# First x rows cast by POOL's queue, and inner products 1 and 5 of four stages split a third time

## The chip, the cores and the metric

The kernel runs on one core of one Trainium2 chip. The time is the device time of one execution in microseconds (us); of three runs the median is 1380.51 us. Five engines work side by side, each on its own instructions in program order, and wait for each other through semaphores: TensorE (PE in the profile, with PEld for loading the stationary operand), VectorE (DVE), ScalarE (ACT), GpSimd (POOL) and SyncE (SP). POOL, SP and ACT also issue the transfers (DMA). Transfers that change the type on their way, from 32-bit to 16-bit floats, are issued by POOL.

## The reference

```python
batch, seq, hidden, n_experts, expert_hidden = 16, 512, 512, 8, 2048
logits_max = np.max(router_logits, axis=-1, keepdims=True)
probs = np.exp(router_logits - logits_max)
probs = probs / np.sum(probs, axis=-1, keepdims=True)
output = np.zeros((batch, seq, expert_hidden), dtype=np.float32)
for e in range(n_experts):
    expert_out = np.matmul(x, expert_weights[e])
    output += probs[:, :, e:e+1] * expert_out
```

That is one product: the left side has 8192 rows and 8 x 512 columns, in which expert e's block is x times that expert's probability; the right side stacks the eight experts' weights to 4096 x 2048.

## The kernel before

**Two levels of splitting.** The product is cut in two along rows, depth and columns, and each such 2 x 2 x 2 cut is done with 7 products instead of 8, from sums and differences of blocks (Strassen's scheme in Winograd's form). The outer level has the products r = 1, 2, 5, 6, 7, 4, 3, each over 16 pieces q of 256 rows, with a depth of 4 experts x 512 and 1024 columns. `product(r, q)` is one such piece. The inner level cuts the piece again: 128 rows, a depth of 1024 (8 chunks of 128, K8), 512 columns (one PSUM bank). Its 7 inner products come in the order `STEPS = (1, 5, 6, 2, 7, 3, 4)`. An inner product is a step of 8 matmuls, each 128 x 128 by 512 columns, that add up in one bank. The 512 rows of the first two pieces of product 1 are computed plainly at the start (lines 316 to 340).

**Stages.** A stage is one or two pieces (`add(...)`, lines 716 to 743), and `run(stage)` (line 689) interleaves their steps: 1a 1b 5a 5b 6a 6b 2a 2b 7a 7b 3a 3b 4a 4b, fourteen slots. Stages 0 to 3 hold pairs of product 1, stages 4 to 9 one of product 2 and one of product 1, stages 10 to 14 pairs of product 2. Two pieces of a stage that belong to one product share the right factor.

**What VectorE does.** For a piece, `Left` makes z (x times probabilities, line 430; twice, for k = 0 and 1), the difference s2 (tile d) and i (from z and d, for inner products 7 and 3). `Right` makes differences of the weights, 128 x 4096 each. After a step, `post` empties or copies the bank: on ScalarE copies, on VectorE additions to a base. A piece of product 2 adds to kept rows: its bases are fetched into the h tiles (12 buffers), or, for q of 9 and more, are the outputs of product 1 still in them. In bank terms inner product 1 ends in bank x, which `post(1)` copies (product 1) or adds to its base (product 2) into bank b; 6, 7 and 4 go on in x, 5 and 3 in bank q, 2 in b.

**What sets the order.** Every instruction from line 342 on is kept in program order. The program itself decides when VectorE does a task: `later(cost, make)` appends to one queue, `slack()` after each step runs tasks while a modelled VectorE clock is behind a modelled TensorE clock, and `need(task)` runs everything queued up to a task that the next step reads. Hooks (`at(stage, slot, make)`) start loads of weights and queue tasks at a slot: in stage 11 from slot 6 `odd_t` queues three weight differences of 2.29 each (line 873), in stages 4 to 9 `wedge_at` queues three of 1.22. Input rows are begun two stages ahead (`start_loads`) and finished by transposing transfers on SP's queue (`finish_loads`).

**The start.** The first 1024 rows of x are in xs0 as 16-bit floats. Its first half comes as 32-bit rows through ScalarE's and SyncE's queues (line 86) and is cast by ScalarE and VectorE (`cast_x32`, line 301); the second half (`cast_x`, line 199) and the weights b11 come through POOL's queue, which casts. `early_z0` multiplies a row block by a diagonal of probabilities on TensorE. Ten matmuls on zeros run ahead of it.

Of the kernel before, what the change touches and what calls it, by code (L numbers as in the profile page):

```python
# [31 lines left out]
def kernel(  # L32
# [7 lines left out]
    nc = tc.nc  # L40
    P = 128
    f16 = mybir.dt.float16
# [64 lines left out]
    def dve(i):  # L107
        last[i.ins.engine] = i.ins
        tc.keep_in_program_order(i)
# [28 lines left out]
    def new_w():  # L138
        return wpool.tile([P, K8, NB], f16, name="w", tag="w")
# [59 lines left out]
    def cast_x(j):  # L199
# [4 lines left out]
    nc.gpsimd.affine_select(out=ident, in_=ident, compare_op=mybir.AluOpType.is_equal, fill=0.0, base=0,  # L204
                            pattern=[[-1, P]], channel_multiplier=1)
    b11 = {kn: new_w() for kn in BLOCKS}
    with behind():
        for kn in BLOCKS[:3]:
            cast_block(11, kn, b11[kn], 2 if kn == (0, 0) else 1)
# [88 lines left out]
                for c in (2 * g, 2 * g + 1) for j in (2 * h, 2 * h + 1)]  # L298
    ORDERS = [(c, j) for c in range(C) for j in range(4)], QUARTERS

    def cast_x32(j):
        if j % 2:
            dve(nc.vector.tensor_copy(xs0[:, j, :], x32[:, j, :]))
        else:
            act(nc.scalar.copy(xs0[:, j, :], x32[:, j, :]))  # L305

    ds_ = [diag_e(0)]
    for h in range(2):
        for j in (2 * h, 2 * h + 1):
            cast_x32(j)  # L310
# [70 lines left out]
    def evacuated():  # L381
        clock["dve"] = max(clock["dve"], clock["pe"]) + 0.69


    x_dram = {}
# [48 lines left out]
    class Left:  # L434
# [6 lines left out]
        def make(self, k):  # L441
            if self.of is not None:
                need(self.of.task[k])
            t = self.t[k] = new_z()
            times(t, k, self.xb, self.pb)
            if self.less is not None:
                u = new_u()
                times(u, k, *self.less)
                tt(t, t, u, SUB)
            if self.of is not None:  # L450
                tt(t, self.of.t[k], t, SUB)
# [99 lines left out]
                tt(o[tn], q if p in (5, 3) else x, o[tn], ADD)  # L551


    def out_rows(q, odd, cols, tn):
        t, n = tn
        return out_f[ds((2 * q + odd) * HQ + t * HP, HP), ds(cols * NH + n * NB, NB)]
# [127 lines left out]
    def queue_lefts(stage):  # L684
        if stage < len(stages):
            for p in stages[stage]:
                queue_left(p.left)

    def run(stage):
        some = stages[stage]  # L690
        for p in some:
            p.left.queue_i()
        n = 0
        for i in range(len(STEPS)):
            for p in some:
                for make in hooks.get((stage, n), ()):
                    make()
                p.step(p.steps[i])
                slack()
                p.post(p.steps[i])  # L700
                n += 1
                if n == 1:
                    queue_lefts(stage + 1)
                if n == late.get(stage, 1):
                    start_loads(stage + 2)
                if n == 5:
                    store_loads(stage + 1)
                if n == 7:
                    finish_loads(stage + 2)

    def fetch_at(stage, slot, base, *tns):
        for tn in tns:
# [334 lines left out]
```

## Time and profile before

| what | us |
|---|---|
| runs: median, lowest, highest | 1380.51, 1379.98, 1381.56 |
| span of the profiled execution | 1380.8 |
| TensorE busy in it | 1370.6 |
| VectorE busy in it | 1109.4 |
| ScalarE, POOL busy in it | 184.2, 410.8 |

The profile gives the span, from the first instruction to the last, as the profiled execution's own time; it lies within the three runs' times. In its rows, a row of the timeline reads: start, duration, engine, line, operation, output tile and input tiles, shapes, count, and in brackets how long the engine had been idle and what ended that. A row of the windows reads: the stretch, its length, each engine's busy time with the number of instructions, the clock that was granted to TensorE (1.00 is full), the transfers' share and their GB/s. A group's row reads: line, engine, operation, tiles, shapes, count, then busy time in us and the mean of one in ns, then the idle time ahead of them.

### The profile page before, as it was taken

To read this page: it belongs to the slowest core of one execution; us is meant where nothing else is said; L and a number is where in the kernel's file an instruction comes from. 1 tells how busy PE (TensorE), PEld (TensorE's weight loads), DVE (VectorE), ACT (ScalarE), POOL (GpSimd) and SP (SyncE) were. 2 spreads that over 40 slices of the span, in tenths; PEclk is the share of its full clock that TensorE was granted. 3 is DMA by queue.
4 is the path that set the end of the run, shared out by engine and by line. 5 is a ranking of instruction groups with operands and counts; after the bars stand their busy time and mean duration, and the time that the engine had idled before them with its cause. 6 is when DMAs were issued, how large, how long until landed. Compare 5 with 4: busy or idle time off the path is not lost.

```text
span 1380.8 us, 17496 instructions
## 1 busy us (share of the span) xinstructions
PE 1370.6 (99%) x6394; PEld 622.9 (45%) x6394; DVE 1109.4 (80%) x1292; ACT 184.2 (13%) x319; POOL 410.8 (30%) x650
## 2 busy tenths in 40 slices
PE   8999999999999999999999999999999999999998
PEld 4444444444444444444444444444444444444444
DVE  5755767769889888789897988889889898898782
ACT  3222111100001111111111100000000000222221
POOL 2122323231223233343332122233333322232321
PEclk9999999999999999999999999999999999999999
DMA  9898999999897998899897998988898979998785
GB/s 194 200 267 196 222 226 279 239 299 370 241 339 231 285 297 261 260 263 250 259 268 267 327 402 216 224 235 211 232 233 229 238 214 313 225 199 184 166 150 99
DMA packets 191287, 338.54 MB, mean 245 GB/s; under 512 B 52961, under 2 KB 87009, under 8 KB 187489
## 3 DMA queue, kind: packets, MB, share of 16 engines
q0 software_dynamic: 88400, 184.59, 55.1%
q1 hardware_dynamic: 98480, 123.86, 30.8%
q10 hardware_dynamic: 4320, 28.98, 5.3%
q8 instruction: 50, 0.82, 0.3%
q14 instruction: 37, 0.29, 0.1%
HBM read 207.65 MB, written 156.43 MB: 264 GB/s over the span
## 4 chain that ended last, share of the span: by engine, by line
PE 91%; issue 4%; DMA 2%; POOL 1%; DVE 1%; ACT 0%; ACTq 0%; POOLq 0%; DVEq 0%
PE ps L134 91%; DMA out_dram<-h 1%; POOL out_dram L128 1%; DVE h L114 1%; DMA x<-in_x_dram 0%; POOL wd L128 0%; DVE z L114 0%; DVE u L114 0%; DVE z L234 0%; ACT w L305 0%; DVE h L188 0%; DVE h L189 0%; DVE h L184 0%; ACT h L186 0%; ACT z L232 0%
## 5 line engine op out<-in xcount | busy, mean ns | idle before, releaser
L134 PE MATMUL ps<-w,z 128*128 128x512 f16 x5416 | 1179.3, 379 | 1.7 <-DVE h L114 1.7
L134 PEld LDWEIGHTS <-z 128*128 128x128 f16 x5416 | 530.1, 98 | 639.7 <-issue 4.5
L128 POOL DMA_DIRECT2D out_dram<-h x380 | 248.9, 676 | 748.6 <-ACT h L544 373.3
L114 DVE TENSOR_TENSOR h<-ps,h 128x512 f32<-128x512 f32 x415 | 282.3, 687 | 210.3 <-PE ps L134 189.6
L114 DVE TENSOR_TENSOR z<-xT,pT 128x2048 f16<-128x2048 f16 x220 | 266.8, 1216 | 11.6 <-DMA xT<-xs 7.2
L134 PE MATMUL ps<-w,d 128*128 128x512 f16 x880 | 199.1, 379 | 0.0
L134 PEld LDWEIGHTS <-d 128*128 128x128 f16 x880 | 86.1, 98 | 103.8
L114 DVE TENSOR_TENSOR z<-z,d 128x2048 f16<-128x2048 f16 x110 | 132.1, 1215 | 0.0
L114 DVE TENSOR_TENSOR w<-w 128x1024 f16<-128x1024 f16 (+2 forms) x92 | 100.8, 1102 | 4.5 <-DMA wd<-w 2.7
L533 ACT COPY h<-ps 128x512 f32<-128x512 f32 x90 | 52.8, 586 | 374.6 <-PE ps L134 321.5
L544 ACT COPY h<-ps 128x512 f32<-128x512 f32 x64 | 37.5, 586 | 486.0 <-PE ps L134 435.6
L114 DVE TENSOR_TENSOR d<-z 128x1024 f16<-128x1024 f16 x110 | 75.3, 685 | 6.8 <-PE ps L134 5.0
L114 DVE TENSOR_TENSOR z<-z,u 128x2048 f16<-128x2048 f16 x64 | 78.4, 1225 | 2.2
L114 DVE TENSOR_TENSOR u<-xT,pT 128x2048 f16<-128x2048 f16 x64 | 77.9, 1217 | 0.0
L530 ACT COPY h<-ps 128x512 f32<-128x512 f32 x90 | 52.8, 587 | 173.9 <-PE ps L134 162.5
L128 POOL DMA_DIRECT2D wd<-w x86 | 48.3, 584 | 35.3 <-DVE w L114 26.2
L128 POOL DMA_DIRECT2D w<-in_expert_weights_dram x65 | 49.1, 784 | 32.4 <-DMA wd<-w 22.6
L114 DVE TENSOR_TENSOR ps<-ps,h 128x512 f32<-128x512 f32 (+1 forms) x66 | 45.3, 688 | 12.6 <-PE ps L134 12.6
L128 POOL DMA_DIRECT2D kept<-h x56 | 30.9, 551 | 77.1 <-ACT h L533 48.3
L114 DVE TENSOR_TENSOR h<-h 128x512 f32<-128x512 f32 (+2 forms) x69 | 45.0, 674 | 0.1
L526 ACT COPY ps<-ps 128x512 f32<-128x512 f32 x45 | 25.6, 570 | 114.6 <-PE ps L134 114.6
L114 DVE TENSOR_TENSOR z<-z 128x2048 f16<-128x2048 f16 x32 | 39.2, 1225 | 1.1
(51 smaller groups left out, 101.2 us busy)
## 6 DMA issues: line engine op xcount, KB each, us to landing
out_dram<-h POOLq DMA_DIRECT2D x380, 256.0 KB, 6.2
pT<-p_dram SPq DMA_DIRECT2D x140, 256.0 KB, 6.0
w<-wd ACTq DMA_DIRECT2D x27, 1024.0 KB, 9.7
h<-kept SPq DMA_DIRECT2D x100, 256.0 KB, 5.6
xT<-x SPq DMA_DIRECT2D x87, 256.0 KB, 5.7
wd<-w POOLq DMA_DIRECT2D x72, 256.0 KB, 5.6
w<-in_expert_weights_dram POOLq DMA_DIRECT2D x35, 512.0 KB, 10.1
h<-out_dram SPq DMA_DIRECT2D x68, 256.0 KB, 5.1
```

What stands on the lines that cost most here:

```text
L114: dve(nc.vector.tensor_tensor(out=o, in0=a, in1=b, op=op))
L128: note(nc.gpsimd.dma_start(out=o, in_=i, **how))
L134: note(nc.tensor.matmul(ps, z, w, start=start, stop=stop, skip_group_check=True))
L526: act(nc.scalar.copy(self.banks["b"], x))
L530: act(nc.scalar.copy(o[tn], q if p == 5 else x))
L533: act(nc.scalar.copy(o[TN[p]], b if p == 2 else x))
L544: act(nc.scalar.copy(o[tn], b))
```

## The change

Two things are changed.

The first half of xs0 is loaded by two casting transfers of POOL's queue, ahead of the weights; the 32-bit tile, its two transfers and its four casts are gone.

In stages 2 and 3 (product 1) and 11 and 12 (product 2) the two pieces' inner products 1 and 5 are done together. The two pieces' row blocks are the two halves of the rows, the depth of 8 chunks is cut in 4 and 4, the 512 columns in 256 and 256, and the 8 block products are replaced by 7 parts of 4 matmuls of 128 x 128 by 256 columns. `Split` makes the four differences of the right factor for each of the two inner products (tile t, once for the two stages), `Third` the four sums of the left side (tile s, for each stage). Within the banks, parts 1 and 5 fill the two halves of the second piece's bank; ScalarE copies one half into the first piece's bank and the other into an h tile; parts 2, 6, 7, 3 and 4 add to halves, and after 6 and 7 VectorE adds 256 columns from a bank and the h tile into a bank. The last two steps (4a, 4b) of the stage ahead are held back and run between the parts; the four posts of 1 and 5 follow the last part. The left sides of such a stage are made in another order: both first z, the four s, both d, both second z.

```diff
-    x32 = wpool.tile([P, 4, H], f32, name="x32", tag="w")
...
-        begin.dma_start(out=x32[:, ds(2 * q, 2), :], in_=x_f[rows, :].rearrange("(p j) h -> p j h", p=P))
...
+    for q in range(2):
+        pool(xs0[:, ds(2 * q, 2), :], x_f[ds(2 * q * HQ, HQ), :].rearrange("(p j) h -> p j h", p=P))
     with behind():
...
-    def cast_x32(j):
-        if j % 2:
-            dve(nc.vector.tensor_copy(xs0[:, j, :], x32[:, j, :]))
-        else:
-            act(nc.scalar.copy(xs0[:, j, :], x32[:, j, :]))
...
+    class Split:
...
+        def make(self, p, i):
+            if i == 0:
+                self.t[p] = wpool.tile([P, 4, C, HQ], f16, name="t", tag="w")
+            w, t = self.right.op(p), self.t[p]
+            block = lambda k, n: w[:, ds(k * C, C), COLS[n]]
+            x, y = ((block(0, 1), block(0, 0)), (block(1, 1), t[:, 0]), (block(1, 1), block(0, 1)),
+                    (block(1, 0), t[:, 1]))[i]
+            tt(t[:, i], x, y, SUB)
...
+    class Third:
...
+        def make(self, i):
+            if i == 0:
+                self.s = wpool.tile([P, 4, C, HQ], f16, name="s", tag="w")
+            s, (a, b) = self.s, (p.left.t[0] for p in (self.a, self.b))
+            lo, hi = ds(0, C), ds(C, C)
+            x, y = ((b[:, lo], b[:, hi]), (s[:, 0], a[:, lo]), (b[:, hi], s[:, 1]), (a[:, hi], s[:, 1]))[i]
+            tt(s[:, i], x, y, ADD if i == 0 else SUB)
...
+        def part(self, p, m):
+            n = "xq"[THIRD.index(p)]
+            if m == 1:
+                self.b.banks[n] = bank()
+            ya, yb = self.a.banks.get(n), self.b.banks[n]
+            z, w = self.op(p, m), self.split.op(p, m)
+            o = {1: (yb, 0), 5: (yb, 1), 2: (ya, 0), 6: (yb, 0), 7: (yb, 0), 3: (ya, 1), 4: (yb, 0)}[m]
+            for c in range(C):
+                mm(o[0][:, COLS[o[1]]], z[:, c], w[:, c], m == 1 and c == 0, c == C - 1)
+            clock["pe"] += 0.44
+            if m == 5:
+                ya = self.a.banks[n] = bank()
+                act(nc.scalar.copy(ya[:, COLS[0]], yb[:, COLS[0]]))
+                self.t5[n] = h_tile([P, HQ], f32)
+                act(nc.scalar.copy(self.t5[n], yb[:, COLS[1]]))
+            elif m in (6, 7):
+                evacuated(0.42)
+                tt((ya if m == 6 else yb)[:, COLS[1]], yb[:, COLS[0]], self.t5[n], ADD)
...
+    def run_third(stage):
+        t = thirds[stage]
+        before(stage, 0)
+        t.parts("x1", "x5", "q1", "q5")
+        after(stage, 1)
+        before(stage, 1)
+        held.pop(0)()
+        after(stage, 2)
+        t.parts("x2", "q2", "x6", "q6")
+        before(stage, 2)
+        held.pop(0)()
+        after(stage, 3)
+        before(stage, 3)
+        t.parts("x7", "q7", "x3", "q3", "x4", "q4")
+        for p in THIRD:
+            for product in (t.a, t.b):
+                product.post(p)
+        after(stage, 4)
...
+    for stage in (2, 3):
+        third(stage, 1)
+    at(1, 2, splits[1].queue)
+    for stage in (11, 12):
+        third(stage, 2)
+    at(10, 2, splits[2].queue)
```

In the names of the parts, x stands for inner product 1 and q for inner product 5, and the digit is the part. With the change the program has 96 matmuls more (224 of 256 columns for 128 of 512), VectorE has 48 operations more and two casts fewer, ScalarE 16 copies of 256 columns more, two casts and one transfer fewer, POOL two transfers more, SyncE one fewer.

More of the change, by code (lines that the diff above doesn't have):

```diff
@@ L379, in slack, with evacuated @@
             queue.popleft().run()
-    def evacuated():
-        clock["dve"] = max(clock["dve"], clock["pe"]) + 0.69
+    def evacuated(cost=0.69):
+        clock["dve"] = max(clock["dve"], clock["pe"]) + cost
     x_dram = {}
@@ L682, in queue_left, with third, before, after @@
             left.queue_make(1)
-    def queue_lefts(stage):
-        if stage < len(stages):
+    thirds, splits, held = {}, {}, []
+    def third(stage, r):
+        if r not in splits:
+            splits[r] = Split(right[r])
+        thirds[stage] = Third(*stages[stage], splits[r])
+    def queue_lefts(stage):
+        if stage in thirds:
+            two = [p.left for p in stages[stage]]
+            for left in two:
+                left.queue_make(0)
+            thirds[stage].queue_sums()
+            for left in two:
+                left.queue_s2()
+            for left in two:
+                left.queue_make(1)
+        elif stage < len(stages):
             for p in stages[stage]:
                 queue_left(p.left)
+    def before(stage, n):
+        for make in hooks.get((stage, n), ()):
+            make()
+    def after(stage, n):
+        if n == 1:
+            queue_lefts(stage + 1)
+        if n == late.get(stage, 1):
+            start_loads(stage + 2)
+        if n == 5:
+            store_loads(stage + 1)
+        if n == 7:
+            finish_loads(stage + 2)
+    def run_third(stage):
[12 more added lines that the diff above has]
+        t.parts("x7", "q7", "x3", "q3", "x4", "q4")
+        for p in THIRD:
+            for product in (t.a, t.b):
+                product.post(p)
+        after(stage, 4)
     def run(stage):
@@ L692, in run, with one @@
             p.left.queue_i()
[L693 to L709, printed above, removed]
+        slots = [(p, i) for i in range(len(STEPS)) for p in some]
+        def one(n):
+            p, i = slots[n]
+            before(stage, n)
+            p.step(p.steps[i])
+            slack()
+            p.post(p.steps[i])
+            after(stage, n + 1)
+        first = 0
+        if stage in thirds:
+            run_third(stage)
+            first = 4
+        end = len(slots) - (2 if stage + 1 in thirds else 0)
+        for n in range(first, end):
+            one(n)
+        for n in range(end, len(slots)):
+            held.append(lambda n=n: one(n))
     def fetch_at(stage, slot, base, *tns):
```

31 lines of the change are left out of this document (29 added, 2 removed).

## The prediction

> **What bounds the kernel now.** I read the page's busy times first, then its chain of waits, then TensorE's groups by form.
>
> ```profile
> span 1380.8 us, 17496 instructions
> PE 1370.6 (99%) x6394; PEld 622.9 (45%) x6394; DVE 1109.4 (80%) x1292; ACT 184.2 (13%) x319; POOL 410.8 (30%) x650
> PE 91%; issue 4%; DMA 2%; POOL 1%; DVE 1%; ACT 0%; ACTq 0%; POOLq 0%; DVEq 0%
> ...
> L134 PEld LDWEIGHTS <-z 128*128 128x128 f16 x5416 | 530.1, 98 | 639.7 <-issue 4.5
> ```
>
> ```profile
> L134 PE MATMUL ps<-w,z 128*128 128x512 f16 x5400 | 1177.5, 379 | 1.7 <-DVE h L114 1.7
> L134 PE MATMUL ps<-w,z 128*128 128x256 f16 x16 | 1.9, 273 | 0.0
> ```
>
> TensorE is busy 99% of the span, and the 5400 large matmuls waited 1.7 us in all. So the end moves by what is added to TensorE's row of work: columns taken out, waits put in. VectorE, at 80%, sets nothing now, but it works in program order, and the change gives it more to do. Where that matters is a question of single stages, so I read windows of one stage's length: one around stage 2, and three across stages 10 to 12.
>
> ```profile
> core 0: us, PE busy (x) PEld busy (x) DVE busy (x) ACT busy (x) POOL busy (x), PEclk, DMA share, GB/s
> 87.00:111.00 24.00, 24.00 (x113) 10.92 (x112) 10.97 (x13) 5.83 (x10) 6.63 (x11) 1.00 1.19 256
> 279.00:303.00 24.00, 24.00 (x113) 10.84 (x111) 18.34 (x23) 1.76 (x3) 9.09 (x15) 1.00 1.10 317
> 303.00:327.00 24.00, 24.00 (x113) 10.90 (x112) 17.91 (x22) 1.17 (x2) 5.89 (x10) 1.00 1.11 312
> 327.00:351.00 24.00, 24.00 (x113) 10.88 (x112) 22.05 (x24) 1.18 (x2) 4.87 (x9) 1.00 1.00 391
> ```
>
> The reader is to see that TensorE has no gap in any of them, and that VectorE has 13 us free around stage 2, 6 us in stages 10 and 11, and 2 us in stage 12. The span is 0.3 us above the median of the runs, 1380.51, so I add changes to the median.
>
> **Columns taken out.** The diff puts four stages (2, 3, 11, 12) on the new scheme, two inner products each: 8 times, two steps of 8 matmuls 512 wide become 7 parts of 4 matmuls 256 wide. One step's length is the distance between VectorE's releases by TensorE near the end; a 256-wide matmul's pitch comes from the group of 16 above.
>
> ```profile
> 1371.81 0.69 DVE L114 TENSOR_TENSOR h<-ps,h 128x512 f32<-128x512 f32 x1 [1.98 <-PE ps L134]
> 1373.54 0.69 DVE L114 TENSOR_TENSOR h<-ps,h 128x512 f32<-128x512 f32 x1 [1.04 <-PE ps L134]
> 1375.26 0.69 DVE L114 TENSOR_TENSOR h<-ps,h 128x512 f32<-128x512 f32 x1 [1.03 <-PE ps L134]
> ```
>
> A step is (1375.26 - 1371.81)/2 = 1.73 us. The 16 matmuls took 1.9 us with the last one's 0.273 in it, so the pitch is (1.9 - 0.273)/15 = 0.108 and a part is 0.43 us. 8 x (2 x 1.727 - 7 x 0.434) = 3.3 us. That group is only 16 matmuls; at a pitch of 0.110 it would be 3.0. I take -3.2, between -3.0 and -3.4.
>
> **What VectorE and ScalarE get.** 16 differences of weights (t), 16 sums of the left side (s) and 16 additions of 256 columns. Prices, as pitch from start to start in a row without idle time:
>
> ```profile
> 295.12 0.69 DVE L114 TENSOR_TENSOR h<-ps,h 128x512 f32<-128x512 f32 x1 [2.73 <-DMA kept<-h]
> 295.73 0.68 DVE L114 TENSOR_TENSOR d<-z 128x1024 f16<-128x1024 f16 x1
> 296.33 0.68 DVE L114 TENSOR_TENSOR h<-ps,h 128x512 f32<-128x512 f32 x1
> 296.93 1.22 DVE L114 TENSOR_TENSOR z<-xT,pT 128x2048 f16<-128x2048 f16 x1
> 298.06 0.68 DVE L114 TENSOR_TENSOR h<-ps,h 128x512 f32<-128x512 f32 x1
> ...
> 327.36 2.28 DVE L114 TENSOR_TENSOR w<-w 128x4096 f16<-128x4096 f16 x1
> ...
> 1365.69 0.76 DVE L114 TENSOR_TENSOR ps<-ps,h 128x256 f32<-128x256 f32 x2 [3.30 <-PE ps L134]
> 1377.01 0.37 ACT L999 COPY h<-ps 128x256 f32<-128x256 f32 x1 [12.42 <-PE ps L134]
> ```
>
> 0.60 for a t, an s or an evacuation h; 1.13 for a product z; 2.20 for a weight sum w (its 2.28 less the 0.08 by which the others overlap); 0.38 for an addition of 256 columns: 32 x 0.60 + 16 x 0.38 = 25 us in all. ScalarE's 16 copies of 0.37 us fall where it is busy 1.2 to 5.8 us in 24; each has a whole held step (1.73 us) before a part needs it. These cost nothing unless h buffers are late. What counts is when TensorE next needs VectorE, and for that I walk the changed program's order with these pitches.
>
> **Stages 2 and 3: no wait.** VectorE makes the second z of stage 2 when its x lands (78.97, below); behind it now stand 4 s, 2 d, 2 z, 6 t and 4 evacuations, and 2 z for stage 2. The pitches sum to 17.1, so the first 256-wide addition can start at 96.1. TensorE ended stage 1's last step before the new parts at 90.2; four parts, a held step, four parts and a held step later, 97.1, it needs that addition, 0.4 us long. Cover: 0.6 us. If the x landed more than 0.6 us later, the rest would go on the path.
>
> ```profile
> 78.97 1.23 DVE L114 TENSOR_TENSOR z<-xT,pT 128x2048 f16<-128x2048 f16 x1 [5.17 <-DMA xT<-xs]
> 90.27 0.69 DVE L114 TENSOR_TENSOR h<-ps,h 128x512 f32<-128x512 f32 x1 [1.04 <-PE ps L134]
> ```
>
> **Stage 11, first use of t for product 5: +1.0.** Before stage 11 VectorE waits for a store of kept rows until 295.12. From there the changed order is
>
> ```
> h(5a) z h(5b) s h(6a) s h(6b) s s d d z z h(7a) t h(7b) t h(3a) t t h(3b) t'
> ```
>
> that is 18 x 0.605 + 3 x 1.13 = 14.3 us up to the first t', which ends at 310.1. TensorE's stage 10 has its first step's end at 288.83, so its twelfth ends at 288.83 + 11 x 1.727 = 307.8, and after three parts, at 309.1, it asks for t'. Wait 1.0. Even without the wait for the store, h(3a) can't start before its step ends at 306.1, and five operations from there end at 309.3: at least 0.2. A store 0.5 us later makes it 1.5.
>
> ```profile
> 288.83 0.70 DVE L114 TENSOR_TENSOR ps<-ps,h 128x512 f32<-128x512 f32 x1 [0.49 <-PE ps L134]
> ...
> 335.99 1.22 DVE L114 TENSOR_TENSOR z<-z,d 128x2048 f16<-128x2048 f16 x1
> ```
>
> **Stage 12: +0.3 and +3.0.** The three weight sums of the odd block (2.28 us each, queued in stage 11) now don't fit there and slip past the third split. Before, the z that products 7 and 3 need was made at 335.99, as the stage began, the weight sums done in the stage ahead. In the changed order one sum stands between the additions of parts 6 and 7: from the end of q6, 0.05 + 0.36 + 2.20 + 0.61 + 0.40 = 3.6, against 1.73 + 4 x 0.43 = 3.46 until x4 needs it: 0.2, and 0.1 more at the next step. The other two stand between the evacuation of 6b and that z: from the end of 6b, 0.05 + 0.61 + 2.31 + 2.20 + 1.22 = 6.4 us, while TensorE has only 2a and 2b, 3.45 us, before 7a needs the z. Wait 3.0. This hangs on no transfer: the evacuation itself waits for TensorE, so nothing earlier can shrink it. Queued behind are 7a and everything after it. One stage later the same order leaves TensorE ahead of every wait by my walk.
>
> **The clock after a 3 us wait: +1.5.** At the start of the kernel the granted clock fell after a patchy stretch:
>
> ```profile
> 7.27 0.62 PE L134 MATMUL ps<-h,w 128*128 128x128 f16 x8 [1.25 <-ACT w L305]
> 9.09 0.86 PE L134 MATMUL ps<-h,w 128*128 128x128 f16 x8 [0.55 <-ACT w L305]
> ...
> 9.00:9.50 0.50, 0.41 (x6) 0.41 (x7) 0.00 (x0) 0.03 (x1) 0.39 (x1) 0.82 1.22 201
> 12.50:13.00 0.50, 0.50 (x4) 0.15 (x2) 0.00 (x0) 0.00 (x0) 0.50 (x1) 0.76 1.26 211
> 31.00:32.00 1.00, 0.55 (x3) 0.06 (x1) 0.54 (x2) 0.63 (x2) 0.00 (x0) 1.00 1.25 205
> 32.00:33.00 1.00, 0.08 (x2) 0.11 (x3) 0.00 (x0) 1.00 (x3) 0.00 (x0) 1.00 0.79 128
> ```
>
> A mean of 0.82 over 9.0 to 9.5 and 0.76 over 12.5 to 13.0 puts half speed from 9.3 to 12.7, 3.4 us. In the 3.4 us ahead of that TensorE had been idle 1.25 + 0.55 us, about half. At 31 to 33 it was idle 0.45 + 0.92 and kept its clock. So some 1.8 us of idleness in one such stretch are enough, 1.4 are not. If the stretches have fixed edges, 3.0 us of waiting put 1.8 into one of them in 0.8 of the positions; then up to 3.4 us run at half speed and cost 1.1 to 1.7, mean 1.5. I take 1.5; the other bound is 0. The Trainium skill ("TensorE: Matmul & The Clock Gate", section "What's actually happening") says that the clock is halved after at least one idle window of about 3.4 us. By that rule a 3.0 us wait costs itself alone; the start of this trace, where no gap is longer than 1.25 us, speaks against it.
>
> **The first rows of x: +0.4.** Two transfers leave the ScalarE and SyncE queues, two enter POOL's ahead of nine weight casts (the first seven issue from 1.47, 0.76 us each). The casts on ScalarE and VectorE go.
>
> ```profile
> 1.47 5.35 POOL L128 DMA_DIRECT2D w<-in_expert_weights_dram  x7
> 8.66 0.72 POOL L128 DMA_DIRECT2D w<-in_x_dram  x1 [1.15 <-DMA w<-in_expert_weights_dram]
> 10.17 3.16 PE L134 MATMUL ps<-w,z 128*128 128x512 f16 x8
> ```
>
> Now TensorE starts on x at 7.27 (above), and the first weight part (256 KB) is there at 8.66. POOL's queue alone moves about 205 GB/s (the 0.5 us rows above): 2.6 us for each 512 KB half of x, 1.3 for that part. No row shows when it starts to move. After the issue of the first transfer, 2.2, at the earliest: x at 4.8 and 7.4, weights at 8.7, where real matmuls start now at 10.17, a gain of 1.4. At the latest the first half takes the 7.2 us that the first weight part took beside x: x at 8.6 and 11.2, weights at 12.5, a loss of 2.3. Half-way the weights land at 10.6: I take +0.4. The later weights (the next experts) keep over 2 us of cover. Kept stores, a weight store and base loads move by a few places in POOL's and SyncE's queues; by the same walk each lands 2 us or more before its use. On ScalarE's queue one weight load must now wait until stage 12 is done with s; behind it stands the copy after 2a, 6 us later.
>
> **Sum.** -3.2 + 1.0 + 0.3 + 3.0 + 1.5 + 0.4 = +3.0: 1383.5.
>
> **Rivals.** A, the forecast: 1383.5, chance 0.45. B, the waits without the fall of the clock: 1382.0, chance 0.27; for it, no row shows how one single long gap is taken; against it, the patchy start above. C, the early start: POOL's queue, with nothing in front of it, moves from 2.2 on, real matmuls begin 1.4 us earlier, and TensorE is busy enough to skip the half-speed stretch (3.4 x 0.5 = 1.7): 1383.5 - 0.4 - 3.1 = 1380.0, not slower. It decides from the point where the first weights land before about 9. Against it: nothing of POOL's had landed before 8.66 though it issued at 1.47. Chance 0.12; where the clock also holds in stage 12 it reaches 1378.5. D, more waits: x of stage 2 or the kept store 1 us later than now, or h buffers late under ScalarE's copies: 1385.5, chance 0.12. E, the scheme doesn't save columns: weight loads of 0.098 us each (the LDWEIGHTS row) stop hiding beside a pitch of 0.108 and nothing is gained: 1386.7, chance 0.04; the 16 matmuls at 0.108 speak against.
>
> **Range and chances.** 0.2% is 2.8 us, about what a measurement tells from no change: below 1377.7 is faster, above 1383.3 slower. A straddles that line, 0.27 above and 0.18 below; B lies within but for 0.03; C within, with 0.04 below; D and E are slower. With some room on the slow side of B and the fast side of C for what I have not seen: faster 0.07, same 0.46, slower 0.47. The likeliest case alone: 1382.4 to 1384.7. Range 1379.8 to 1385.5: E, and what of C and D lies beyond, is left out.
>
> **What would show it.** In stage 12 one TensorE gap of about 3 us, released by VectorE's z from z and d, with the granted clock at half for up to 3.4 us behind it; a gap of about 1 us in stage 11 released by a t; 14 parts of 0.43 us in each third split; no gap in stages 2 and 3; the first real matmul near 10.6. Wrong if VectorE's two weight sums do not precede that z in time, if TensorE's idle sum stays under 2 us, or if the parts take over 0.46.

## The result and the profile after

| | us |
|---|---|
| before: median, lowest, highest of 4 runs on the same chip | 1381.03, 1379.98, 1381.57 |
| after: median, lowest, highest of 4 runs | 1386.29, 1384.13, 1387.99 |
| ratio, 95% interval | 1.0039, 1.0027 to 1.0051 |
| spans of the four runs after | 1382.4, 1384.0, 1385.2, 1386.3 |
| profiled executions: span before, after | 1380.8, 1382.4 |

The changed kernel is 5.3 us slower; 3.0 were forecast, and 1386.29 lies above the range. Two things stand out. In every run after, the time is the span plus 1.7, so the profiled execution of before, span 1380.8, took about 1382.5: above the runs of its table, not among them. And the profiled execution of after is the fastest of its four. Two profiles whose spans are 1.6 apart stand for medians 5.3 apart.

TensorE's rows of the profile after, all gaps from 296 to 352 us:

```profile
306.41 0.60 PE L132 MATMUL ps<-t,s 128*128 128x256 f16 x4 [1.03 <-DVE t L112]
309.83 0.60 PE L132 MATMUL ps<-w,z 128*128 128x256 f16 x4 [0.66 <-ACT ps L615]
338.40 1.03 PE L132 MATMUL ps<-t,z 128*128 128x256 f16 x8 [0.25 <-DVE ps L112]
349.39 2.85 PE L132 MATMUL ps<-w,z 128*128 128x512 f16 x8 [2.99 <-DVE z L112]
```

The forecast's waits are there almost to the digit: 1.03 for t, 0.25 for the addition, 2.99 for z at 7a. The second row was not in its sum: TensorE waits for ScalarE. ScalarE's and VectorE's rows of the same execution say what is late:

```profile
305.03 0.36 ACT L615 COPY ps<-ps 128x256 f32<-128x256 f32 x1 [7.25 <-PE ps L132]
309.13 0.37 ACT L617 COPY h<-ps 128x256 f32<-128x256 f32 x1 [3.75 <-DMA out_dram<-h]
309.40 0.38 ACT L615 COPY ps<-ps 128x256 f32<-128x256 f32 x1
```

```profile
319.77 0.69 DVE L112 TENSOR_TENSOR h<-ps,h 128x512 f32<-128x512 f32 x1 [1.67 <-DMA h<-kept]
...
343.59 4.61 DVE L112 TENSOR_TENSOR w<-w 128x4096 f16<-128x4096 f16 x2
348.12 2.35 DVE L112 TENSOR_TENSOR z<-z,d 128x2048 f16<-128x2048 f16 x2
```

The copy that saves a half bank needs an h buffer, and this one is free only when its old contents have been stored (out_dram<-h); the copy for the next inner product stands behind it and TensorE behind that. VectorE waits 1.67 for a kept base that came late into another h buffer; in this execution that wait does not reach TensorE, whose gaps are the four above. The last two rows are the forecast's two weight sums ahead of z.

The windows around the 2.99 wait (stretch, length, busy time of TensorE, its weight loads, VectorE, ScalarE, POOL with counts, then the granted clock):

```profile
346.78:350.19 3.41, 0.80 (x4) 0.41 (x5) 3.41 (x3) 0.24 (x1) 0.99 (x2) 1.00 1.00 401
350.19:353.60 3.41, 3.41 (x10) 1.18 (x8) 2.71 (x4) 0.00 (x0) 0.33 (x1) 0.50 0.48 165
```

One stretch at half clock, 1.7 us lost. The parts cost what was forecast (groups of TensorE by shape: 0.273 each, overlapping at a pitch of 0.108):

```profile
L132 PE MATMUL ps<-t,s 128*128 128x256 f16 x96 | 13.1, 273 | 1.0 <-DVE t L112 1.0
...
L132 PE MATMUL ps<-w,s 128*128 128x256 f16 x32 | 4.1, 273 | 0.0
```

### The profile page after: what moved, and what is told of

It is laid out like the page before. It is cut to its first block, busy times and chain, and to the rows that moved or that the text cites. A ratio compares the mean times of both kernels' runs of the same rounds, so it can differ in the third digit from the quotient of the medians.

```text
span 1382.4 us, 17755 instructions
## 1 busy us (share of the span) xinstructions
PE 1368.2 (99%) x6490; PEld 632.1 (46%) x6490; DVE 1134.2 (82%) x1338; ACT 187.8 (14%) x333; POOL 411.5 (30%) x652
## 4 chain that ended last, share of the span: by engine, by line
PE 66%; issue 5%; POOL 2%; DMA 1%; DVE 1%; POOLq 0%; ACT 0%; DVEq 0%
PE ps L132 66%; POOL out_dram L126 2%; DMA out_dram<-h 1%; DVE w L112 0%; DVE z L112 0%; DVE h L112 0%; POOL wd L126 0%; POOL w L126 0%; DVE u L112 0%; POOLq L126 0%; ACT h L1121 0%; DVEq L112 0%
## 5 line engine op out<-in xcount | busy, mean ns | idle before, releaser
L132 PE MATMUL ps<-w,z 128*128 128x512 f16 x5352 | 1161.4, 378 | 6.1 <-DVE z L112 3.0
L112 DVE TENSOR_TENSOR ps<-ps,h 128x512 f32<-128x512 f32 (+1 forms) x82 | 51.6, 638 | 17.0 <-PE ps L132 17.0
## 6 DMA issues: line engine op xcount, KB each, us to landing
w<-in_expert_weights_dram POOLq DMA_DIRECT2D x35, 512.0 KB, 10.2
```

The lines of the kernel that those rows point to most:

```text
L112: dve(nc.vector.tensor_tensor(out=o, in0=a, in1=b, op=op))
L132: note(nc.tensor.matmul(ps, z, w, start=start, stop=stop, skip_group_check=True))
```

## The experiments

All kernels have ScalarE's 252 copies of a full bank into an h tile in the same order. The table gives, for one profiled execution each, how much later such a copy starts than the same copy in the profile of before (copies at 32, 149, 413, 893 and 1364 us there: after the start, after stage 3, behind stages 11 and 12, after the stretch near 800, near the end), and the timed ratio with its interval. The medians and ratios are of all timed executions; the profile shows one of them.

```
                    32     149     413     893    1364   median   ratio  interval
changed kernel    -2.07   -3.66   +2.09   +2.10   +1.95  1386.29  1.0039 1.0027-1.0051
repeat            -1.78   -2.92   +3.27   +3.83   +3.35  1386.47  1.0035 1.0023-1.0048
start_only        -1.81   -1.81   -1.81   -1.22   -0.77  1381.49  0.9997 0.9988-1.0006
p1_only           +0.23   -1.36   -1.36   -1.19   -1.70  1379.62  0.9989 0.9980-0.9998
start_p1          -1.72   -1.88   -1.88   -1.78   -1.92  1379.92  0.9987 0.9978-0.9996
thirds_only       -1.59   -2.42   +4.14   +5.64   +4.99  1385.42  1.0030 1.0019-1.0042
own_t5            -0.48   -1.82   +1.11   +2.34   +3.63  1386.15  1.0030 1.0019-1.0042
odd_late          -1.55   -2.42   -1.50   +3.25   +2.42  1385.42  1.0028 1.0016-1.0041
thirds_1011       -1.65   -3.06   +0.93   +1.43   +1.10  1383.92  1.0020 1.0011-1.0028
keep_clock        -1.36   -2.94   +1.49   +2.65   +2.17  1386.75  1.0030 1.0019-1.0042
early_z           -1.63   -1.88   +2.05   +4.16   +4.04  1384.88  1.0022 1.0013-1.0030
early_z_t5        -1.78   -3.37   +0.79   +2.33   +1.73  1384.11  1.0017 1.0008-1.0026
early_z_t5_start  -1.53   -1.46   +3.27   +4.64   +4.40  1386.64  1.0032 1.0023-1.0042
t_early           -1.69   -2.75   +7.96   +9.06   +7.84  1384.25  1.0022 1.0005-1.0039
t_early_t5        -0.88   -0.46   +0.89   +2.68   +2.36  1382.06  1.0005 0.9995-1.0015
s11_t5            -1.89   -3.16   -2.63   -1.93   -2.16  1380.68  0.9990 0.9981-0.9998
t_early_start     -1.62   -3.21   -1.33   -0.77   +0.45  1385.77  1.0023 1.0013-1.0034
h_free            -1.70   -3.17   -3.29   +1.81   +0.60  1383.60  1.0017 1.0005-1.0028
x9                -1.79   -3.38   -1.29   +1.38   +0.17  1385.17  1.0030 1.0016-1.0044
```

The kernel before had a median of 1381.03 beside the first row and of 1381.8 to 1382.2 beside the others.

### Which part loses: the start, stages 2 and 3, or stages 11 and 12

`repeat` is the changed kernel. `start_only` has only the first part of the diff, `p1_only` only stages 2 and 3, `start_p1` both, `thirds_only` all four split stages with the old start. What `p1_only` and `start_p1` leave out:

```diff
-    for stage in (11, 12):
-        third(stage, 2)
-    at(10, 2, splits[2].queue)
```

> The changed kernel again, unchanged. What is open: its median stands 5.3 us above the kernel before (1386.29 against 1381.03), while the two profiled executions differ by 1.6 (1382.4 against 1380.8). Theory R (what varies from execution to execution is stage 11 and 12: how much of the waiting hits the clock, and how late the store is that keeps the h buffer): the median comes out at +4 to +6 again and the spans spread over 3 us or more, while the spans of the kernel before, from the same chip, spread under 2 and lie at 1378 to 1380.5. Rival S (the profiled execution of the kernel before was one with a slow start, its other executions start 2 us faster, so the change gains nothing at the start): the same +4 to +6, but the spans of both kernels spread alike, and the run that changes the start alone shows no gain. Rival N (the 5.3 is the lot of one session): +1 to +3.

> The kernel before with the first rows of x cast by POOL's queue, and no third split. In the changed kernel's profile the fourth of the real start (a mark that both have, 32.92 before) came at 30.85: 2.07 earlier, of which about 1.3 from the clock that stayed at 1.00 between 6 and 18 us. Theory (the start is as good as that in most executions): 2.1 below the kernel before, -1.5 to -2.5. Rival S (the profiled start of the kernel before was a bad one): -0.8 to 0. Step of the prediction (weights land at 10.6): +0.4.

> The kernel before with the third split in stages 2 and 3 alone, the start as before. The changed kernel's trace shows no wait in those two stages and parts of 0.43 us. Theory (columns are saved there and nothing is paid): -1.6, that is half of 3.15, between -1.3 and -1.9. Rival (the four sums and four differences for each push later VectorE work past its time, or ScalarE's copies of 256 columns hold h buffers): -0.5 to +1.5, with a wait in stages 3 to 5 that the kernel before does not have.

> The changed kernel without the split in stages 11 and 12: new start, stages 2 and 3 split. Theory (all the loss sits in stages 11 and 12): -1.6 from the columns and -0.8 to -2.1 from the start, so -2.4 to -3.7, and spans that spread no more than those of the kernel before; it would beat both kernels. Rival (part of the loss comes with the start or with stages 2 and 3): -1 to +2, with spans that spread over 3 us.

> All four third splits, the start as before. From the drift of the copies in the changed kernel against the kernel before: -3.66 at the end of stage 3, +2.09 at 413 us, so stages 11 and 12 cost 5.75 there (6.19 in the second profile of the changed kernel). Theory (the loss sits in stages 11 and 12 and does not depend on the start): stages 2 and 3 give -1.6 (timed alone: -2.2), so +3.5 to +4.6 against the kernel before, with waits of about 3.0 for z, 0.25 for ps and 0.3 to 1.0 for t, 0.7 to 1.8 for ScalarE's copy, and 3.4 us at half clock behind the 3.0. Rival (the old start leaves the h buffer's store more time, so the wait for the copy goes): +2.5 to +3.

The repetition stands at 1.0035. Its spans, and those of the kernel before beside it, spread alike (3.5 us each), as rival S said. Splitting stages 2 and 3 gains (0.9989), by 1.59 in the trace as forecast; stages 11 and 12 turn -2.42 into +4.14 in `thirds_only`. The start shows no gain in time (0.9997, again rival S, though the interval leaves room for 1.7 us), and the clock tells why. Windows of before, then of early_z, which has the same old start:

```profile
5.91:9.32 3.41, 1.61 (x16) 0.89 (x16) 1.50 (x3) 1.72 (x3) 2.26 (x4) 1.00 1.18 182
9.32:12.74 3.42, 3.42 (x15) 1.46 (x13) 1.91 (x5) 0.59 (x1) 1.08 (x3) 0.50 1.24 207
```

```profile
6.11:9.52 3.41, 1.65 (x18) 1.05 (x19) 1.45 (x3) 1.72 (x3) 2.12 (x3) 1.00 1.18 185
9.52:12.93 3.41, 3.41 (x33) 2.11 (x31) 2.88 (x7) 1.33 (x3) 1.34 (x2) 1.00 1.24 207
```

1.80 us idle against 1.76 decide over 1.7 us. Of the 13 profiles with the old start two fell (before and p1_only); of the 7 with the new one none. Where the clock held, the old start stands at -0.48 to -1.89 in the first column (mean 1.5) and the new at -1.36 to -2.07 (mean 1.7): most of the 2.07 is the 1.7 of a clock that usually held anyway. Even the 0.2 between the means comes from own_t5 and t_early_t5, where the clock first rose to full only at 10.9 and 10.3 us (in the other eighteen at 4.7 to 7.3): until then matmuls of 512 columns started 0.427 apart, after it 0.216. Without these two both means are 1.7.

`start_p1` shows what an early start meets. TensorE's and VectorE's rows in stage 2:

```profile
89.67 0.60 PE L132 MATMUL ps<-t,s 128*128 128x256 f16 x4
91.00 2.76 PE L132 MATMUL ps<-w,z 128*128 128x512 f16 x16 [0.73 <-DVE h L112]
...
96.60 1.03 PE L132 MATMUL ps<-t,s 128*128 128x256 f16 x8 [0.25 <-DVE ps L112]
```

```profile
79.00 1.22 DVE L112 TENSOR_TENSOR z<-xT,pT 128x2048 f16<-128x2048 f16 x1 [6.59 <-DMA xT<-xs]
```

Where VectorE waits for it, the x of stage 2 lands at 76.2 to 80.4, with the new start (77.0 to 79.4) no earlier than with the old one; TensorE is there 1.7 us sooner than with a fallen clock. In before's pace (landing less the first column) it came at 79.09 in the changed kernel, 79.73 in the repetition, 80.06 in thirds_only, 80.72 here; the copy at 99 us shows that TensorE lost 0, 0.45, 0.76 and 1.43 more in stage 2 than in the changed kernel: all that lies beyond 79.29. `start_p1` so gains 0.13% (1.8 us) and not the 2.4 to 3.7 expected.

### What the wait for z costs: the clock, and the weight sums ahead of it

`keep_clock` puts eight matmuls that nothing reads into the gap; `odd_late` moves the weight sums out of it:

```diff
+    def busy():
+        o, w = bank(), stages[12][0].left.t[0]
+        for i in range(8):
+            mm(o, w[:, i, ds(0, P)], right[2].op(1)[:, i], True, True)
+    at(12, 8, busy)
```

```diff
-    at(11, 6, odd_t)
+    at(12, 5, odd_t)
...
-    sums_at(12, 8, 5, t1, (5, 6))
-    sums_at(13, 2, 5, t1, (7, 4))
+    sums_at(13, 4, 5, t1, (5, 6))
+    sums_at(13, 11, 5, t1, (7, 4))
...
-    at(10, 2, splits[2].queue)
+    at(9, 3, splits[2].queue)
```

> The changed kernel with eight matmuls of 128 x 128 by 512 columns (8 x 0.216 = 1.73 us) into a bank of their own that nothing reads, ahead of 7a in stage 12, where TensorE otherwise waits 3.0 for z. What the profiles so far show: the clock record has edges every 3.413 us, and a stretch between two edges with 1.80 us or more of TensorE idle was followed by one at half clock (before, the split in stages 2 and 3 alone, both changed kernels, all four splits, the late differences, stages 10 and 11), one with 1.70 or less was not; the same 3.0 us wait, cut by an edge into 1.69 and 1.31, cost no clock in the run with the half bank's own buffer. Theory (idle time within one such stretch decides, more than some 1.75): the wait shrinks to 1.3, no half clock behind it, 7b and everything behind 1.7 us earlier, so 1.2 to 1.7 below the changed kernel in the median (+3.0 to +3.5 against the kernel before). Rival (the half clock comes from the wait for z as such or from VectorE's lateness): the wait for z and the half clock stay, no gain.

> thirds_only, with VectorE's three weight differences of 2.29 us queued in stage 12 at slot 5 and not in stage 11 at slot 6, the sums for outer product 5 moved behind them (stage 13, slots 4 and 11), and the right differences t queued at slot 3 of stage 9. Theory (the 3.0 us wait for z is those weight differences ahead of it, and the clock falls because of it): no wait for z nor ps nor t in stages 11 and 12, no half clock there, so 3.0 + 0.25 + 1.0 + 1.7 = 6 less; but VectorE has no idle time to make it up in stages 13 to 15 and a wait of 2.0 for z comes in stage 15, so 3.5 to 4.5 less than thirds_only, about level with the kernel before. Rival (VectorE's total work is the limit there and the wait only moves): 0.5 to 1.5 less than thirds_only, with 3 us or more of waiting in stages 13 to 15.

In `keep_clock` the wait is 1.26, and no stretch of the kernel before its tail runs at half:

```profile
350.48 5.79 PE L132 MATMUL ps<-w,z 128*128 128x512 f16 x26 [1.26 <-DVE z L112]
```

In `odd_late` the wait for z left stage 12 and came back in stage 15, with the half clock, though it is only 2.06 long. Row and windows:

```profile
439.50 5.75 PE L134 MATMUL ps<-w,z 128*128 128x512 f16 x18 [2.06 <-DVE z L114]
```

```profile
436.37:439.78 3.41, 1.35 (x7) 0.46 (x6) 3.41 (x5) 0.59 (x1) 0.56 (x1) 1.00 0.51 60
439.78:443.19 3.41, 3.41 (x10) 1.22 (x9) 1.78 (x3) 0.00 (x0) 0.00 (x0) 0.50 1.05 290
```

The same 3.0 us wait cost no clock in `own_t5`, where an edge cut it:

```profile
345.38:348.79 3.41, 1.73 (x8) 0.59 (x6) 3.38 (x2) 1.17 (x2) 1.62 (x3) 1.00 1.00 390
348.79:352.20 3.41, 2.10 (x10) 0.99 (x11) 3.41 (x4) 0.00 (x0) 0.00 (x0) 1.00 0.98 392
```

So the mechanism is shown in the traces. The times did not follow: `keep_clock` (1.0030) was expected 1.2 to 1.7 us below the changed kernel and `odd_late` (1.0028) 3.5 to 4.5 below thirds_only, and neither moved measurably.

### What else is in stages 11 and 12: the h buffers

`own_t5` gives inner product 1's saved half bank a buffer outside the h tiles; `thirds_1011` moves the split stages to 10 and 11; `early_z` asks for stage 12's first z before slot 10 of stage 11; `early_z_t5` and `early_z_t5_start` add the buffer and the new start. In the second cut the last line belongs to the three `early_z` kernels alone.

```diff
-                self.t5[n] = h_tile([P, HQ], f32)
+                if n == "x":
+                    self.t5[n] = t5pool.tile([P, HQ], f32, name="t5", tag="t5")
+                else:
+                    self.t5[n] = h_tile([P, HQ], f32)
```

```diff
-    for stage in (11, 12):
+    for stage in (10, 11):
         third(stage, 2)
-    at(10, 2, splits[2].queue)
+    at(9, 3, splits[2].queue)
+    at(11, 10, lambda: [need(p.left.task[0]) for p in stages[12]])
```

> thirds_only, but the third split's saved half bank of inner product 1 has a buffer of its own and not one of the 12 h buffers (inner product 5's still takes one; the router's start logits take h buffers instead). Theory (TensorE's wait for ScalarE's copy in stage 11 comes from the copy ahead of it, which waits for an h buffer whose store to the output is not done): that wait of 0.7 to 1.8 is gone, so 0.7 to 1.8 less than thirds_only, and no new wait larger than 0.3 in its place. Rival (the second copy takes the same late buffer, and its wait reaches TensorE by the addition after part q6): 0 to -0.4.

> thirds_only, with product 2's two split stages one earlier, 10 and 11 in place of 11 and 12, and the right differences t queued at slot 3 of stage 9. The same columns are saved. VectorE was busy 16.6 of 24 us at 256 to 280 and 20.8 at 280 to 304 in the changed kernel, against 22.5 of 26 in stage 12. Theory (the loss is where the split stages meet the three weight differences): waits of at most 0.3 for VectorE, no half clock, so -3.2 from the columns plus 0 to 1.8 for h buffers: -3.2 to -1.4 against the kernel before, faster than both. Rival (a split stage of product 2 costs VectorE more than it has, wherever it stands): +1 or more, with waits for VectorE of over 2 us somewhere from stage 10 to 15.

> thirds_1011, and in stage 11 ahead of slot 10 VectorE is made to produce the first z of stage 12's two pieces (there VectorE idled 3.7 us for TensorE while that z was still queued, then TensorE waited 2.6 for it and the clock fell for 3.4 us). Theory: those 2.6 + 1.7 = 4.3 go and nothing comes in their place; what is left beside the columns (-3.2) is the wait for ScalarE's copy (1.0 there): 4.0 to 4.3 less than thirds_1011, so about -2 against the kernel before. Rival (VectorE is the limit and falls behind in stages 13 to 15): 1 to 2.5 less than thirds_1011, with a wait of 2 us or more there.

> early_z with the saved half bank of inner product 1 in a buffer of its own, as in own_t5. Theory: no wait for ScalarE's copy in stage 11 (0.7 to 2.3 in the runs so far, 0 in own_t5), so 0.7 to 2.0 less than early_z, about -3 against the kernel before. Rival (the wait only passes to an addition or to the next h buffer): within 0.5 of early_z.

> early_z_t5 with the first x rows cast by POOL's queue, that is the changed kernel with two split stages moved, z earlier and the half bank in a buffer of its own. Theory (the start alone brought 0.3 in time: what it gains is partly chance, as the old start's clock fell in two of six profiled executions, and partly paid back in stage 2, where x lands when it landed): 0 to 0.8 less than early_z_t5. Rival (the start really gains 2): 1.5 to 2.1 less.

In `own_t5` TensorE's wait for the copy is gone from the trace, the time is not shorter. `thirds_1011` was expected to beat both kernels and came out at 1.0020, with a wait of 2.57 for z, as its rival said. `early_z` was aimed at the wrong z: its wait of 2.4 stayed, and VectorE's rows show that it is for a z of stage 11 itself, behind two additions:

```profile
320.88 1.38 DVE L114 TENSOR_TENSOR h<-ps,h 128x512 f32<-128x512 f32 x2 [3.41 <-DMA h<-kept]
322.17 1.21 DVE L114 TENSOR_TENSOR z<-xT,pT 128x2048 f16<-128x2048 f16 x1
```

The first addition waited for a base that landed at 320.8; the second needs the step that TensorE ended at 321.08. From there the second addition and z take 0.05 + 0.61 + 1.22, so with the base in time about 1.9 of the 2.4 would be left: most of this wait is VectorE's order, the base's share about 0.5. `early_z_t5` stands 0.8 below early_z, within the noise. `early_z_t5_start`, expected 0 to 0.8 below early_z_t5, stands 2.5 above it; in its profile stage 2 loses 1.7 (x at 79.43), and VectorE waits 4.50 for the base where it was 3.92.

Why bases are late shows when they are fetched. The trace's issue and landing of three of the fetches that SyncE's queue makes, counted from the first kept base, and where `h_free`, below, has them:

```
fetch        before           after            repeat           h_free
 8th    300.4 to 306.0   296.1 to 301.5   296.0 to 301.7   296.8 to 302.2
10th    311.6 to 318.8   316.6 to 319.6   317.5 to 321.0   310.1 to 317.2
17th    328.9 to 338.0   333.3 to 341.3   333.5 to 342.0   328.5 to 338.6
```

The tenth leaves 5 us later than before, and the landing at 319.6 is what ends VectorE's 1.67 in the profile after. Each split stage of product 2 takes two more h tiles (`h_free`'s expectation says four, wrongly), so later tiles get other buffers, and a fetch waits until the last use of its buffer is over. In the profile after, the tenth waited for an addition of VectorE that ended at 316.55, the 17th for a store that left at 325.49 and landed at 333.28. The last experiments test that. `t_early` is `thirds_only` with the one slot `at(9, 3, splits[2].queue)`; `t_early_t5` adds own_t5's buffer, `s11_t5` then drops stage 12's split, `t_early_start` is the slot in the changed kernel. `h_free` is `t_early` with both half banks in buffers of their own, for which one of ten x buffers goes; `x9` is that loss alone.

> thirds_only with the right differences t for product 2 queued at slot 3 of stage 9, not slot 2 of stage 10. VectorE then does them where it idles (16.6 of 24 us busy), one of the three weight differences of 2.29 comes back into stage 11, and one, not two, stands ahead of z in stage 12: its wait falls from 3.0 to about 0.8, below what drops the clock; no wait for t. Theory (the loss is the sum of the waits): 2.2 + 1.7 + 0.8 = 4.7 less than thirds_only, which is level with the kernel before or up to 1 below. Rival (a split stage of product 2 costs 2 to 3 us whatever its waits): the waits go as said, the time falls by less than 2.

> t_early with the saved half bank of inner product 1 in a buffer of its own. Theory: ScalarE's wait for the h buffer goes as well, 0.7 to 2.3 less than t_early: -1 to -3 against the kernel before, the fastest of all together with the split of stages 2 and 3 alone. Rival: within 0.5 of t_early.

> t_early_t5 without the split in stage 12: three split stages, none beside the three weight differences. Theory: no wait over 0.3 from stage 10 to 15, and columns of three stages: 0.8 less than the split of stages 2 and 3 alone (-1.7 on the mean), so about -2.5 against the kernel before. Rival (a split stage of product 2 costs in any case): 0 to +2, with the loss at stage 11 or where transfers are the limit, near 800 us.

> The changed kernel with the right differences t for product 2 queued at slot 3 of stage 9, nothing else. Theory: the same 4.7 less than the changed kernel (+4.8 on the mean): level with the kernel before, -0.8 to +0.8, with ScalarE's wait of 0.7 to 2.3 left in stage 11. Rival: +2.5 to +4.

> t_early with both saved half banks of a third split in two buffers of their own (9 x buffers for 10 make the room). Theory (four more h tiles for each split stage of product 2 push its base fetches and copies behind stores that free a buffer 8 to 12 us after their issue): ScalarE's wait for stores ahead of the half bank's copies gone, VectorE's waits for kept bases under 0.5, TensorE left with about 1.3 us for VectorE in stage 12, so -2.4 (columns) + 1.3 = about -1 against the kernel before, 3 to 4 less than x9 on the mean, with a spread of about 1 and not 4. Rival (the lack is of transfer time, not of buffers): within 1 of x9.

> t_early with 9 x buffers for 10 and nothing else. Theory: as t_early, +2 to +4 against the kernel before, with ScalarE's and VectorE's waits for stores and kept bases of 3 to 5 us in stages 11 and 12; one x buffer less costs under 1. Rival (x buffers are as short as h buffers): over 2 more than t_early.

The order did what was said: in `t_early_t5` and `t_early_start` the wait for z is 0.67. In `t_early`'s profiled execution it was 4.45, because the base came last. VectorE, then TensorE:

```profile
350.14 0.69 DVE L114 TENSOR_TENSOR h<-ps,h 128x512 f32<-128x512 f32 x1 [4.02 <-DMA h<-kept]
350.75 2.28 DVE L114 TENSOR_TENSOR w<-w 128x4096 f16<-128x4096 f16 x1
352.94 1.22 DVE L114 TENSOR_TENSOR z<-z,d 128x2048 f16<-128x2048 f16 x1
```

```profile
354.22 2.32 PE L134 MATMUL ps<-w,z 128*128 128x512 f16 x5 [4.45 <-DVE z L114]
```

That base, the 18th, left at 337.7 (335.1 before) and landed at 350.0, 12.3 later; in the other kernels' profiles it took 6.7 to 10.2. `t_early`'s twelve times run from 1381.6 to 1395.9; that such landings make the difference is likely, but only one of the twelve was profiled. `t_early_t5` came out level with the kernel before (1.0005) where 1 to 3 us less were expected, and `t_early_start` at 1.0023, as its rival said, although its profiled execution (1382.63, median 1385.77) shows neither the 3.0 us wait nor a half clock. In `h_free` ScalarE's copies follow TensorE at once, and VectorE waits for no kept base from 296 to 356:

```profile
305.51 0.36 ACT L624 COPY ps<-ps 128x256 f32<-128x256 f32 x1 [7.25 <-PE ps L135]
305.78 0.38 ACT L626 COPY t<-ps 128x256 f32<-128x256 f32 x1
306.39 0.36 ACT L624 COPY ps<-ps 128x256 f32<-128x256 f32 x1 [0.23 <-PE ps L135]
306.66 0.38 ACT L626 COPY t<-ps 128x256 f32<-128x256 f32 x1
```

From the copy at 149 to that at 413, between which only stages 11 and 12 differ, `h_free` then gains 0.12 in the trace, and `x9`, its control, loses 2.09. The 2.2 between them are TensorE's wait of 1.85 for ScalarE's copy with 0.16 for the broken row (see below), and 0.2 of wait for an addition. So in the trace the cause of ScalarE's wait and of the late bases is shown. In time it is not: `h_free` lies 1.8 below x9 on the mean, with 3 to 4 expected and under 1 by the rival, and its times spread over 7.7 us, not 1. The h buffers' share of the changed kernel's time is so not measured. In its profile 5.1 us are lost again between 413 and 893 (a wait of 2.24 near 820 and the half clock behind it); `x9` loses 2.7 there, with the same wait. In time `x9` stands 0.9 above t_early, which is near what was expected and within the noise. Where no stage of product 2 is split (before, start_only, p1_only, start_p1), no profile shows a wait for a kept base there, and none of ScalarE's copies starts later than TensorE lets it (one row of start_only names a store, but after the same 21.86 us of idle time as before the change). `s11_t5`, with one such stage, is the only kernel with one that gains, 0.10% (1.4 us, where 2.5 were expected), and no more than `p1_only`.

## Why the prediction was wrong, point by point

- **Columns, parts, z, addition:** right, to 0.1. **E** (no columns saved) falls. **The wait for t:** 1.03, and 0.31 in the repetition, where TensorE came later; within its bounds.
- **The clock:** +1.5 against 1.7, by the mechanism forecast, fixed stretches and 1.8 us of idle. B's case, the wait without the fall, was seen once, in `own_t5`, by luck of where the edge fell.
- **The failed step** is "by the same walk each lands 2 us or more before its use", with the h buffers' copies left at nothing ("These cost nothing unless h buffers are late"). Kept bases between 296 and 356 us end a wait of VectorE of 0.3 to 4.5 us in 12 of 16 profiles with a split stage of product 2, and ScalarE waits for a store in 15 of them, all but `h_free`. The walk followed engines and queues but not which buffer each tile gets. Rival D named this and priced it at 2.0; it is no rival but one more term: TensorE's wait for ScalarE alone was 0.66 in the first profile and 1.83 in the repetition, and a late base goes on top in some executions (in neither profile of the changed kernel). "This hangs on no transfer" held for the wait of 3.0 only as long as the base was in time (`t_early`).
- **A size missing from every wait:** the forecast's waits, like a row's bracket, begin where the matmul before ends, 0.379 us after its start (the mean in its group's row). In an unbroken row the next one starts after 1.727/8 = 0.216, so each break costs 0.16 more than its bracket; for 256 columns, 0.273 against 0.108, it is as much. The three forecast waits lost 0.5 by that, the four real ones 0.65. It closes the trace: from the copy at 149 to that at 413 the changed kernel loses -1.6 + 4.93 (the four brackets) + 0.65 + 1.7 (the clock) = 5.7, and the table says 5.75.
- **Stages 2 and 3, cover 0.6:** the walk was right and the cover 0.3, but x lands anywhere from 76.2 to 80.4, and where it is late the cover is gone: stage 2 lost 0.45 in the repetition, 1.4 in `start_p1` and 2.0 in `t_early_t5`, by the same count.
- **The start, +0.4:** wrong in the trace by 2.5. The first real matmul came at 9.36, not near 10.6, and the clock held, so C came true in part: not by its 1.4 us, and its own sign, weights before about 9, was missed. But with the old start and a clock that rose as early and held, that matmul came at 9.5 to 9.9 too; in time no gain shows (0.9997).

```profile
9.36 1.89 PE L132 MATMUL ps<-w,z 128*128 128x512 f16 x8 [0.87 <-DMA w<-in_expert_weights_dram]
```

- **Own time:** the span was taken as the execution's time. In all runs the time is 1.65 to 2.8 above the span, so before's profiled execution took longer than any run of its table, and its half-speed stretch is missing in 11 of the 13 profiles with its start. That flatters the changed kernel in the two profiles, not the forecast, which was added to the median.

With the terms of its own profile the changed kernel's sum is -3.2 + 4.93 + 0.65 + 1.7 - 0.2 for the start = 3.9 us, against 5.3 in time; the repetition's is -3.2 + 5.38 + 0.65 + 1.7 + 0.45 in stage 2 - 0.2 = 4.8, against 4.7. The two profiled executions took 2.2 and 0.9 us less than the medians of their runs, and what the others add no trace shows: that stays open. Later bases in some executions would fill it, and so would waits for weights between 800 and 835, 0.2 to 1.8 in all in 12 of the 16 profiles with a split stage of product 2 and in one of the four without; what makes those weights late was not tried. Open too is why taking away one wait at a time (`own_t5`, `keep_clock`, `odd_late`) moved no time measurably. An effect of 1.3 us is about what their six runs, 3 to 4 us apart, can just not tell; for `odd_late` the trace shows that the wait only moved. So the cause is shown for the profiled executions, and only argued for the medians.

The split of stages 2 and 3 beats both kernels: 0.11% under the kernel before (0.02 to 0.20) alone, 0.13% (0.04 to 0.22) with the new start.

## What to carry to other kernels

A walk of the changed order must give each new tile a buffer from its pool and ask when that buffer's last use, a store or an addition, is over, not only which engine comes when: two more short-lived tiles in a pool of 12 moved a fetch by 5 us. Add to each wait of TensorE what its broken row costs, 0.16 here. Take one profile as one draw, add what lies around its span, and look whether its clock fell where other executions' does not before a difference of 2 us is read from two of them. A split stage that gains 0.8 of columns paid here where VectorE had 13 of 24 us free (stages 2 and 3), and not where it had 2 to 6 (stages 10 to 12).

## What the runs showed of the hardware

In all 20 profiles the granted clock changes only at edges that lie on one grid of 3.413 us. A stretch between two edges in which TensorE was idle for 1.80 us or more (13 of them ahead of the kernels' tails, up to 3.18) was followed by one at half clock, 1.78 or less (13 from 1.54 up) was not; one of 1.81 without a fall lies in the tail of start_only, among short matmuls. After one stretch at half, 1.27 us of idle in it was followed by another (t_early). The Trainium skill ("TensorE: Matmul & The Clock Gate", section "What's actually happening") has the stretch of 3413 ns and its free running, which the trace agrees with; but it asks for a whole idle window, and here about half of one was enough, so that a wait of 2.06 cost 3.9 by the copies around it (odd_late) and one of 3.0, cut by an edge, 3.1 (own_t5).
